# Matmul with rotary embedding on one core: how far ahead of the matmuls tiles are cast and transposed

## The chip, the cores and the metric

The kernel runs on one core of one Trainium2 chip. The metric is the device time of one execution in microseconds (us), taken as the median of several runs. Engines go by the profile's names: PE is TensorE (PEld its weight loads), DVE is VectorE, ACT is ScalarE, POOL is GpSimd, SP is SyncE, whose queue issues most loads. A "q" behind an engine's name is its sequencer, which issues DMAs and waits on semaphores.

## The reference

```python
batch, seq, hidden, n_heads = (16, 512, 768, 12)
y = np.matmul(x, weight)                       # x: 16 x 512 x 768, weight: 768 x 768, float32
y = y.reshape(batch, seq, n_heads, head_dim)   # head_dim = 64
y1, y2 = y[..., :32], y[..., 32:]
out1 = y1 * cos1 - y2 * sin1                   # cos, sin: seq x 64, halves taken the same way
out2 = y2 * cos2 + y1 * sin2
out = np.concatenate([out1, out2], axis=-1)    # back to 16 x 512 x 768
```

## The kernel before

**Tiles and pairs.** The 16 x 512 rows of x are cut into 64 tiles of 128 rows. Two tiles of the same rows in neighbouring batches make a pair, since they share their cosines and sines: 32 pairs (`NP`), pair n holding tiles 2n and 2n+1. In the main loop `i = 2 * n + s` is the tile whose matmuls are being issued.

**The way of a tile.** A tile of x is loaded, brought to float16 (the cast), transposed so that the 768 columns that are summed over lie on partitions (the "turn"), multiplied with the weights on PE into PSUM, multiplied on DVE with cosines and sines (`rope_bank`, line 187), added up on POOL (`add`, line 204) and stored (line 249). Loading, casting and transposing take one of three ways, by pair:

- Pairs 8, 12, 16, 20, 24 (`BLOCKS`): POOL's queue loads four quarters straight to float16 (`xh`, line 99), and DVE transposes them in blocks (line 148). There is no cast.
- Pairs 6, 10, 14, 18, 22, 26, 28 (`BLOCKS_SP`): SP's queue loads four quarters as float32 (`xf`, line 99), ACT casts each tile (line 76), and DVE transposes.
- All other pairs: SP's queue loads each tile (`xs`, line 83), ACT casts it, PE transposes it in six steps against an identity matrix (line 140) into PSUM (`pt`), and ACT copies that to SBUF (`xT`, line 76 again: one helper issues casts and copies).

So from pair 6 to pair 28 odd pairs go through PE and even ones through DVE.

**Order.** The kernel writes its own order (`manual_schedule`): on each engine instructions run in the order in which the code issues them. In the main loop, after the matmuls of tile i, `upto("turn", i + 3)` issues transpositions until those of all tiles below i+3 have been issued, and `upto("cast", i + 5)` does the same for casts; both do so once i is over 6 (before that, in pairs 2 and 3, calls with i+2 and i+4 stand between two halves of a tile's matmuls). For a tile that PE transposes, `turn` issues six transposes on PE and the copy on ACT; for the others, one transposition on DVE. Then come the products on DVE, and after the second tile of a pair the store of pair n-3 on ACT's queue and the addition of pair n on POOL. For the last four pairs (`ALONE`) the two `upto` calls stand before the tile's matmuls, and products, additions and stores go in smaller pieces.

**Loads and stores.** At pair n the SP queue is given the loads of pair n+5 and quarters of pairs n+5 to n+8. Buffers: 10 tiles of `xs`, 2 pairs of `xf`, 6 cast tiles `xc`, 8 transposed tiles `xT`, 2 PSUM banks for transposes and 6 for products, 3 pairs of products `tq`, 6 pairs of results `ov`. In the built program the DMAs of SP and ACT take eight completion semaphores in turn; each waits until the DMA that had its semaphore before has landed.

Of the kernel before, what the change touches and what calls it, by code (L numbers as in the profile page):

```python
# [17 lines left out]
def kernel(  # L18
# [21 lines left out]
    NP = B * SB // 2  # L40
# [46 lines left out]
    def load_pair(n):  # L87
        for s in (0, 1):
            if n < NP and n not in BLOCKS and n not in BLOCKS_SP:
                load(n, s)  # L90
# [10 lines left out]
    def load_blocks(n, quarters):  # L101
        if n not in BLOCKS:
            return
        if quarters[0] == 0:
            xhs[n] = bpool.tile([P, 2, H], FP16, tag="xh", name="xh")
            x16[n, 0], x16[n, 1] = xhs[n][:, 0], xhs[n][:, 1]
        for q in quarters:
            load_quarter(n, q, nc.gpsimd, xhs[n])

    def load_blocks_sp(n, q):  # L110
        if n not in BLOCKS_SP:
            return
        if q == 0:
            xhs[n] = hpool.tile([P, 2, H], FP32, tag="xf", name="xf")
            xss[n, 0], xss[n, 1] = xhs[n][:, 0], xhs[n][:, 1]
        load_quarter(n, q, nc.sync, xhs[n])
# [11 lines left out]
    def cast(n, s, eng):  # L128
        xc = cpool.tile([P, H], FP16, tag="xc", name="xc")
        x16[n, s] = xc  # L130
        src = xss.pop((n, s))
        src = src.rearrange("p (m t e) -> p t m e", t=NT, e=2)
        copy(eng, xc.rearrange("p (t m e) -> p t m e", t=NT, e=2), src)

    def transpose(n, s, eng):
        xc = x16.pop((n, s)).rearrange("p (t m e) -> p t e m", t=NT, e=2)
        bank = pt_pool.tile([P, 8, P], FP16, tag="pt", name="pt")
        pt = bank[:, 0 : 2 * NT].rearrange("p (t e) m -> p t e m", e=2)
        for t, e in CHUNKS:
            nc.tensor.transpose(pt[:, t, e, :], xc[:, t, e, :], ident)  # L140
        xT = tpool.tile([P, NT, 2, P], FP16, tag="xT", name="xT")
        copy(eng, xT, pt)
        xTT[n, s] = xT

    def transpose_blocks(n, s):
        order = "p (j a t) -> p t j a" if n in BLOCKS else "p (t j a) -> p t j a"
        xT = tpool.tile([P, NT, P, 2], FP16, tag="xT", name="xT")
        nc.vector.transpose(  # L148
            out=xT.bitcast(FP32).rearrange("p t (j a) o -> p t j (a o)", j=NQ),
            in_=x16.pop((n, s)).bitcast(FP32).rearrange(order, j=NQ, t=NT),  # L150
        )
        xTT[n, s] = xT.rearrange("p t m e -> p t e m")
# [4 lines left out]
    def psum(n, s):  # L157
        key, banks = (n, 3) if n < NP - ALONE else ((n, s), 2)
        if (n, s) == (NP - 1, 1):
            key, banks = (n, s), 3  # L160
        if key not in psys:
            psys[key] = [
                py_pool.tile([P, 512], FP32, tag="psy", name="psy") for _ in range(banks)
            ]
        ps = psys[key]
        if n >= NP - ALONE:
            cuts = (0, HH, H) if banks == 2 else (0, 5 * D, 10 * D, H)
            return [(b[:, 0 : hi - lo], lo, hi) for b, lo, hi in zip(ps, cuts, cuts[1:])]
        cut = 512 if s == 0 else 256
        return [(ps[s][:, ds(s * 256, cut)], 0, cut), (ps[s + 1][:, 0 : H - cut], cut, H)]  # L170

    def mm(n, s, t, e, c0=0, c1=H):
        for k, (ps, lo, hi) in enumerate(psum(n, s)):
            a, z = max(c0, lo), min(c1, hi)
            if a >= z:
                continue
            nc.tensor.matmul(  # L177
                ps[:, a - lo : z - lo],
                xTT[n, s][:, t, e, :],
                w_sb[:, t, e, a:z],  # L180
                start=((t, e) == CHUNKS[0] and n > 1),
                stop=((t, e) == CHUNKS[-1] and (n > 1 or s >= k)),
            )
# [11 lines left out]
    def rope(n, c0, c1, ps):  # L195
        if n not in tqs:
            tqs[n] = rpool.tile([P, 2, 2 * H], FP32, tag="tq", name="tq")
            ovs[n] = opool.tile([P, 2 * H], FP32, tag="ov", name="ov")
        products(n, ps, tqs[n][:, :, c0:c1])
# [11 lines left out]
    def rope_bank(n, b):  # L211
        rope(n, b * 512, (b + 1) * 512, psys[n][b])

    def add_pair(n, step=2 * H):
        for c in range(0, 2 * H, step):
            add(n, c, c + step, nc.gpsimd)
# [8 lines left out]
    def rope_last(n, ps, c0, c1):  # L225
        nh = (c1 - c0) // D
        q = tqs[n][:, 1, c0:c1]
        ph = ps.rearrange("p (h d) -> p h d", d=D)
        for o, j in ((q.rearrange("p (h d) -> p h d", d=D), 1), (ph, 0)):
            nc.vector.tensor_tensor(  # L230
                out=o, in0=ph, op=MULT,
                in1=csn[:, j, n % SB, :].unsqueeze(1).broadcast_to((P, nh, D)),
            )
        nc.vector.tensor_tensor(
            out=ovs[n][:, c0:c1].rearrange("p (h t d) -> p h t d", t=2, d=HD),
            in0=ps.rearrange("p (h t d) -> p h t d", t=2, d=HD),
            in1=q.rearrange("p (h t d) -> p h t d", t=2, d=HD)[:, :, ::-1, :],
            op=ADD,
        )

    def store(n, eng, c0=0, c1=2 * H):
        b, r = where(n, 0)
        dst = out.rearrange("b (p r) h -> r p b h", r=SB)[r, :, b : b + 2]
        src = ovs[n].rearrange("p (b h) -> p b h", b=2)
        if c1 - c0 < 2 * H:
            s = c0 // H
            dst = dst[:, s, c0 - s * H : c1 - s * H]
            src = src[:, s, c0 - s * H : c1 - s * H]
        eng.dma_start(out=dst, in_=src)
# [43 lines left out]
    def upto(what, k):  # L293
        while done[what] < min(k, 2 * NP):
            n, s = divmod(done[what], 2)
            done[what] += 1
            if what == "cast":
                if n not in BLOCKS:
                    cast(n, s, nc.scalar)
            elif n in BLOCKS or n in BLOCKS_SP:  # L300
                transpose_blocks(n, s)
            else:
                transpose(n, s, nc.scalar)
# [46 lines left out]
    for n in range(2, NP):  # L350
        load_pair(n + AHEAD - 2)
        for q, ahead in ((0, 8), (2, 7), (1, 6), (3, 5)):
            if n + ahead >= AHEAD:
                load_blocks_sp(n + ahead, q)
        for m, quarters in ((n + AHEAD_B, (0, 2)), (n + AHEAD_B - 1, (1, 3))):
            if m > BLOCKS[0]:
                load_blocks(m, quarters)
        for s in (0, 1):
            i = 2 * n + s
            if n < 4:  # L360

                for c0, c1 in ((0, 256), (256, H)):
                    for c in CHUNKS:
                        mm(n, s, *c, c0, c1)
                    if c0 == 0:
                        upto("turn", i + 2)
                        upto("cast", i + 4)
            elif n < NP - ALONE:
                for c in CHUNKS:
                    mm(n, s, *c)  # L370
            upto("turn", i + 3 if i > 6 else 0)
            upto("cast", i + 5 if i > 6 else 0)
            if n < NP - ALONE:
                for b in ((0,), (1, 2))[s]:
                    rope_bank(n, b)
                continue
            for ps, lo, hi in psum(n, s):
                for c in CHUNKS:
                    mm(n, s, *c, lo, hi)
                c0, c1 = s * H + lo, s * H + hi  # L380
                if (n, s, hi) == (NP - 1, 1, H):
                    rope_last(n, ps, c0, c1)
                    store(n, nc.sync, c0, c1)
                    continue
                rope(n, c0, c1, ps)
                if n >= NP - 2:
                    add(n, c0, c1, nc.gpsimd)
                elif hi == H:
                    add(n, s * H, (s + 1) * H, nc.gpsimd)
                if (n, s) == (NP - 1, 1):  # L390
                    if lo:
                        store(n, nc.scalar, s * H, c1)
                elif hi == H:
                    store(n, nc.sync, s * H, (s + 1) * H)
        if n < NP - ALONE:
            if n >= 3:
                store(n - 3, nc.scalar)
            add_pair(n, H if n >= NP - ALONE - 2 else 2 * H)
        if n == NP - ALONE - 1:
            for m in (n - 2, n - 1, n):  # L400
                store(m, nc.sync)
# [34 lines left out]
```

## Time and profile before

| | |
|---|---|
| time of five runs | 154.01 to 155.01 us, median 154.09 us |
| the profiled execution | 154.09 us, span 152.3 us |
| PE busy | 145.2 us, 95% of the span |
| DVE busy | 130.9 us, 86% |
| POOL busy | 123.7 us, 81% |
| ACT busy | 73.5 us, 48% |
| chain that ended last | PE 86%, POOL 7%, DVE 3% |
| matmuls (line 177) | 787 records, 131.4 us |
| transposes on PE (line 140) | 240, 20.3 us |
| copies `xT` on ACT | 38, 800 ns each |
| casts `xc` on ACT | 38 from `xs` at 904 ns, 14 from `xf` at 907 ns |
| transpositions on DVE (line 148) | 14 at 562 ns, 10 at 701 ns |
| granted PE clock | 1.00 in each stretch looked at between 16 and 140 us |
| data moved | 51.17 MB, 336 GB/s on average |

The span is the time from the first to the last instruction that the profile shows; the rest of the execution's time lies around it. Busy matmul time is that of records that overlap, so the sum over a row's instructions can be more than the row's busy time. A line such as "ACT xT L76 <- PE pt L140: 53.8, 34, 3.9" says that ACT's copies of line 76 waited for PE's transposes of line 140: 53.8 us in total, 34 times, 3.9 us at the longest. In a line of the chain the first number is the start in us, the second the duration, then engine, tile, line and count. In the timeline the bracket behind a row holds the engine's idle time before it and what ended that.

### The profile page before, as it was taken

What the parts mean: (1) busy time and instruction counts of PE and PEld (TensorE: products, weight loads), DVE (VectorE), ACT (ScalarE), POOL (GpSimd) and SP (SyncE); (2) the same over time, 40 slices, a digit from 0 to 9 for tenths busy, and PEclk for the clock granted to TensorE, in tenths of its full rate; (3) what the DMA queues carried; (4) which work ended last, traced back from release to release, by engine and by line L of the source; (5) the groups of instructions that cost most, each with busy time, mean ns of one, the idle gap of its engine ahead of it and who ended that gap; (6) DMA issues with size and microseconds to landing.
All of it is one profiled execution on the core that took longest, in us unless ns stands there. A gap on an engine that the chain in (4) does not pass through costs nothing.

```text
span 152.3 us, 2731 instructions
## 1 busy us (share of the span) xinstructions
PE 145.2 (95%) x1044; PEld 92.5 (61%) x1044; DVE 130.9 (86%) x141; ACT 73.5 (48%) x91; POOL 123.7 (81%) x69
## 2 busy tenths in 40 slices
PE   6999999999999999999999999999999999999950
PEld 2455678666656666666656666666656666666640
DVE  0566999779898989989898989989898989997890
ACT  3350696883534726282525624582616547764200
POOL 1000399999998999799997999787897879999990
PEclk9999999999999999999999999999999999999996
DMA  5999999999999999999999999999999999996554
GB/s 152 365 404 397 402 309 213 270 369 352 318 334 400 325 316 362 336 401 337 364 316 333 348 365 300 355 402 415 312 360 408 404 411 387 408 355 266 219 203 151
DMA packets 29037, 51.17 MB, mean 336 GB/s; under 512 B 7264, under 2 KB 14944, under 8 KB 29024
## 3 DMA queue, kind: packets, MB, share of 16 engines
q1 hardware_dynamic: 16640, 29.04, 56.7%
q10 hardware_dynamic: 6944, 19.99, 33.3%
q0 software_dynamic: 5440, 1.97, 10.7%
q8 instruction: 8, 0.13, 0.3%
q14 instruction: 5, 0.04, 0.1%
HBM read 27.79 MB, written 25.17 MB: 348 GB/s over the span
## 4 chain that ended last, share of the span: by engine, by line
PE 86%; POOL 7%; DVE 3%; POOLq 1%; issue 0%; DVEq 0%
PE psy L177 75%; PE pt L140 8%; POOL ov L204 7%; PE psy L259 3%; DVE tq L187 1%; DVE xT L78 1%; DVE xc L78 1%; POOLq L431 1%; DVE cold L266 0%; DVE w_sb L126 0%; POOLq L204 0%; DVEq L187 0%
## 5 line engine op out<-in xcount | busy, mean ns | idle before, releaser
L177 PE MATMUL psy<-w_sb,xT 128*128 128x256 f16 (+3 forms) x787 | 131.4, 322 | 0.2 <-DVE w_sb L126 0.2
L187 DVE TENSOR_TENSOR tq<-psy,csn 128x1024 f32<-128x1024 f32 (+2 forms) x100 | 112.1, 1163 | 9.5 <-PE psy L177 9.1
L204 POOL TENSOR_TENSOR ov<-tq 128x1536 f32<-128x1536 f32 (+3 forms) x42 | 111.5, 2680 | 7.9 <-DVE tq L187 5.2
L177 PEld LDWEIGHTS <-xT 128*128 128x128 f16 x787 | 75.2, 98 | 44.8 <-ACT xc L76 0.5
L76 ACT COPY xT<-pt 128x768 f16<-128x768 f16 x38 | 30.4, 800 | 57.9 <-PE pt L140 53.8
L76 ACT CAST xc<-xs 128x768 f16<-128x768 f32 x38 | 33.0, 904 | 9.7 <-DMA xs<-in_x_dram 7.6
L140 PEld LDWEIGHTS <-xc 128*128 128x128 f16 x240 | 17.0, 99 | 6.0 <-DVE xc L78 1.1
L140 PE MATMUL pt<-ident,xc 128*128 128x128 f16 x240 | 20.3, 221 | 0.3 <-DVE xc L78 0.3
L336 POOL COPY mark<-xs 128x1 f32<-128x1 f32 x1 | 0.2, 184 | 16.0 <-DMA xs<-in_x_dram 16.0
L76 ACT CAST xc<-xf 128x768 f16<-128x768 f32 x14 | 12.7, 907 | 0.0
L99 POOL DMA_DIRECT2D xh<-in_x_dram x20 | 11.8, 595 | 0.5 <-issue 0.5
L148 DVE STREAM_TRANSPOSE xT<-xc 128x384 f32<-128x384 f32 x14 | 7.9, 562 | 0.0
L259 PE MATMUL psy<-cold 128*128 128x512 f16 x17 | 6.5, 533 | 1.2 <-DVE cold L266 1.2
L148 DVE STREAM_TRANSPOSE xT<-xh 128x384 f32<-128x384 f32 x10 | 7.0, 701 | 0.0
L126 DVE CAST w_sb<-w_raw 128x768 f16<-128x768 f32 (+2 forms) x7 | 3.4, 501 | 1.9 <-DMA w_raw<-in_weight_dram 1.9
L78 DVE CAST xc<-xs 128x768 f16<-128x768 f32 x2 | 1.9, 947 | 2.9 <-DMA xs<-in_x_dram 2.9
L259 PEld LDWEIGHTS <-cold 128*128 128x128 f16 x17 | 2.0, 131 | 3.5 <-issue 2.2
L78 DVE COPY xT<-pt 128x768 f16<-128x768 f16 x2 | 1.1, 558 | 1.9 <-PE pt L140 1.9
L76 ACT ACT_TABLE_LOAD x1 | 1.3, 1283 | 0.7 <-PEq L417 0.7
L266 DVE MEMSET cold<- 128x256 uint32 x1 | 0.3, 272 | 0.9 <-PEq L417 0.9
L267 POOL MEMSET ident<- 128x128 f16 x1 | 0.2, 204 | 0.3 <-POOLq L417 0.3
L331 DVE COPY csn<-sin_sb 128x128 f32<-128x128 f32 x1 | 0.2, 226 | 0.2 <-DMA sin_sb<-in_sin_dram 0.2
(9 smaller groups left out, 1.8 us busy)
## 6 DMA issues: line engine op xcount, KB each, us to landing
out_dram<-ov ACTq DMA_DIRECT2D x25, 768.0 KB, 8.5
xs<-in_x_dram SPq DMA_DIRECT2D x40, 384.0 KB, 9.0
xf<-in_x_dram SPq DMA_DIRECT2D x28, 192.0 KB, 10.7
out_dram<-ov SPq DMA_DIRECT2D x7, 384.0 KB, 2.3
out_dram<-ov SPq DMA_DIRECT2D x3, 768.0 KB, 6.2
w_raw<-in_weight_dram SPq DMA_DIRECT2D x5, 384.0 KB, 6.8
xh<-in_x_dram POOLq DMA_DIRECT2D x20, 96.0 KB, 10.1
out_dram<-ov ACTq DMA_DIRECT2D x1, 320.0 KB, 2.2
```

The source lines that it names most:

```text
L76: eng.copy(out=o, in_=i_)
L78: eng.tensor_copy(out=o, in_=i_)
L99: eng.dma_start(out=dst[ts(q, R)], in_=src[r, q])
L126: nc.vector.tensor_copy(out=w_sb[:, t, e, c0:c1], in_=w_raw[t, e][:, c0:c1])
L140: nc.tensor.transpose(pt[:, t, e, :], xc[:, t, e, :], ident)
L148: nc.vector.transpose(out=xT.bitcast(FP32).rearrange("p t (j a) o -> p t j (a o)", j=NQ), in_=x16.pop((n, s)).bitcast(FP32).rearrange(orde ...
L177: nc.tensor.matmul(ps[:, a - lo : z - lo], xTT[n, s][:, t, e, :], w_sb[:, t, e, a:z], start=((t, e) == CHUNKS[0] and n > 1), stop=((t, e) ...
L187: nc.vector.tensor_tensor(out=tq.rearrange("p j (h d) -> p j h d", d=D), in0=ps.rearrange("p (h d) -> p h d", d=D) .unsqueeze(1).broadcast ...
L204: eng.tensor_tensor(out=ovs[n][:, ds(c0, w)].rearrange("p (h t d) -> p h t d", t=2, d=HD), in0=tq[:, 0].rearrange("p (h t d) -> p h t d", ...
L259: nc.tensor.matmul(psys[n][b], cold[:, 0:P], cold, start=True, stop=opened[0] < WARM - 6)
L266: nc.vector.memset(cold, 0.0)
L431: with _tile.TileContext(nc) as tc:
```

## The change

The two `upto` calls of the main loop get a lead that depends on the tile:

```diff
                 for c in CHUNKS:
                     mm(n, s, *c)
-            upto("turn", i + 3 if i > 6 else 0)
-            upto("cast", i + 5 if i > 6 else 0)
+
+            lead = 1 if i < 2 * NP - 20 else 0
+            upto("turn", i + 3 + lead if i > 6 else 0)
+            upto("cast", i + 5 + 2 * lead if i > 6 else 0)
             if n < NP - ALONE:
```

`2 * NP - 20` is 44. For i from 7 to 43 transpositions are issued up to tile i+3 instead of i+2 and casts up to tile i+6 instead of i+4. From i = 44, which begins the last ten pairs, the limits are those of before; the counters stand at tiles 46 and 49 by then, so the next transposition is issued at i = 45 and the next cast at i = 46. At i = 7, where the lead begins, two transpositions (tiles 9 and 10) and three casts (tiles 11, 12, 13) are issued together, where there were one and one. Nothing else in the kernel is changed; `upto` skips casts of pairs that need none.

## The prediction

> **What bounds the kernel now.** I read the waits of TensorE first, then the chain that ended last, then ScalarE's timeline where the change begins, then the queue of loads.
>
> ```profile
> span 152.3 us, 2731 instructions
> PE psy L259 <- DVE cold L266: 1.2, 1, 1.2
> PE pt L140 <- DVE xc L78: 0.3, 1, 0.3
> PE psy L177 <- DVE w_sb L126: 0.2, 1, 0.2
> ...
> 25.69 0.34 PE pt L140 x6
> 26.03 1.29 PE psy L177 x6
> 27.32 0.34 PE pt L140 x6
> 27.66 1.95 PE psy L177 x12
> ...
> 135.28 1.87 DVE tq L187 x2
> ...
> 130.56 18.16 POOL L204 TENSOR_TENSOR ov<-tq 128x768 f32<-128x768 f32 x14 [0.31 <-POOL ov L204]
> ```
>
> The three waits are all that TensorE has, and the timeline puts each of them before 9.2 us. From there to 146.9 us it strings 1.95 us of matmuls per tile and 0.34 us of transposes per tile of an odd pair without a hole. Pairs 6 to 28 alternate, so two pairs take 8 x 0.975 + 2 x 0.34 = 8.47 us, 4.23 a pair. The tail hangs on it: DVE's products of pair 27 follow its last matmul at 129.3, GpSimd's additions start at 130.56 and run 18.16 us without idling to 148.72, and one store and the end follow (152.3). ScalarE is busy 48% of the span. Its waits show where it has room:
>
> ```profile
> ACT xT L76 <- PE pt L140: 53.8, 34, 3.9
> ACT xc L76 <- DMA xs<-in_x_dram: 7.6, 2, 4.6
> ACT xT L76 <- DMA xf<-in_x_dram: 4.1, 1, 4.1
> ```
>
> 53.8 us are copies waiting for TensorE, and only the last row (and one of 2.0) is a stall on a DMA in the body.
>
> **The change part by part.** No instruction is added or removed: both kernels build to the same number on every engine. Three things move. Below, T(k) is the transposition of tile k (line 140 on TensorE, 148 on DVE) and i the tile whose matmuls the loop is at.
>
> *The step at i=7.* Here the lead jumps, and tile 7 gets T(9), T(10) and the casts of 11, 12, 13 at once, where it had T(9) and cast 11. ScalarE's own order there was:
>
> ```profile
> 26.06 0.80 ACT L76 COPY xT<-pt 128x768 f16<-128x768 f16 x1 [0.70 <-PE pt L140]
> 26.76 0.92 ACT L76 CAST xc<-xs 128x768 f16<-128x768 f32 x1
> 27.69 0.80 ACT L76 COPY xT<-pt 128x768 f16<-128x768 f16 x1
> 27.78 0.42 ACTq L249 DMA_DIRECT2D out_dram<-ov  x1
> 28.39 0.90 ACT L76 CAST xc<-xs 128x768 f16<-128x768 f32 x1
> ```
>
> These are the copy of 8, the cast of 10, the copy of 9, the store of pair 0 and the cast of 11. TensorE finishes T(9) at 27.16 + 0.34 = 27.49 and now has T(10) next, whose cast ends at 27.68. From a cast's end to its first transpose the trace shows 0.06 (DVE's cast 6.79 + 0.94, transposes at 7.79), so T(10) starts at 27.74: 0.25 us of stall. T(10) takes 0.34, tile 8's matmuls 1.95: 30.03. T(11) needs cast 11, which now stands behind the copy of 10. Rows follow each other on ScalarE at 0.70 for a copy: 27.69, copy of 10 at 28.39, cast 11 from 29.09 to 29.99, release 30.05: 0.02. **Sum 0.27 us**. The trace has no T(10) here. Its bounds are 0, if the cast ends 0.25 us sooner, and 0.52, if both waits cost the 0.26 that stands before the transposes at 7.79. A gain is excluded: TensorE's work is the same, and it has no idle time after 9.2 us to give back. I take 0.27.
>
> Behind it, casts 12 and 13 wait for the last quarter of pair 6, which landed at 30.40 in the trace. They run 30.4 to 32.1, and the copy of 11 to about 32.9. Tile 11's matmuls start at 34.3, so 1.4 us of cover remain; past it each us of a late landing is a us of TensorE. The store of pair 0 goes out at about 31.3 instead of 27.78. GpSimd wants its buffer back at pair 6, about 43.3; with the longest landing of a store, 11.0 us, it is there at 42.3.
>
> *Casts two tiles earlier, pairs 6 to 23.* A cast waits for its load, and on ScalarE the copies and stores stand behind it. SyncE's and ScalarE's DMAs share eight completion semaphores in turn, and nearly every one is issued the moment the one eight before it lands (pair 15's second tile at 52.83, its predecessor landed at 52.81), so loads can't simply come 4.2 us earlier. How near they are, from the landings of the trace: the last quarter of pair 10 at 44.40, cast at 47.67; of pair 14 at 60.71, cast at 64.61; pair 15 at 63.82, cast from 67.69; pair 18 at 77.11, cast at 81.65; pair 23 at 95.33, cast from 101.57. With two tiles (about 4.2 us) less, ScalarE meets several loads that have not landed. Tile 28 (pair 14): T(23) ends about 55.9 instead of 57.6, its copy starts at 56.0, casts 26 and 27 run to 58.4, and cast 28 would wait to 60.71, so 2.3 us. What hides it: the copy behind it is of T(26), which TensorE does at 61.8 and which is needed by tile 26's matmuls at 66.1 + 0.27 = 66.4. So cast 28 may start as late as 66.4 - 0.8 - 0.9 = 64.7, 4.0 us after that landing. Cost 0.
>
> Take it from a rule instead: the Trainium skill ("DMA: Bandwidth & Descriptors", section "Rules for kernel authors") says to issue a DMA early, compute, and wait on its semaphore late; this change waits earlier. Counting the 2.3 us above as lost, the rule would make the sum 154.09 + 0.27 + 2.3 = 156.7 for one such cast. The row speaks for 154.4, because a copy with 4.0 us to spare stands between the waiting cast and TensorE.
>
> *Stores.* In ScalarE's new order the store of an even pair from pair 4 on stands behind a copy and follows TensorE: pair 4's goes from 41.39 to about 46.2, pair 8's from 58.41 to about 63.0, pair 6's from 52.00 to about 54.0; odd pairs' stay within a us or go earlier. GpSimd needs the buffers six pairs on: pair 10's addition at 59.9 against 46.2 + 11.0 (longest landing) = 57.2, pair 14's at 76.8 against 74.0. So 2.7 us of cover; without it GpSimd, with 3.47 us of additions and on average 0.6 of DMA issues in 4.23, has 0.16 a pair to recover. A late store also holds its semaphore: pair 4's now stands ahead of pair 15's second tile, which goes from 52.83 to about 46.2 + 10 = 56 and lands near 67, where its cast is due at about 66. Other loads gain: with the store of pair 0 out of the way those of pairs 7 to 10 are issued up to 2.7 us earlier (pair 7's second tile at 20.3, when its new predecessor lands, instead of 22.99). I take these as cancelling.
>
> *Transposes one tile earlier.* On TensorE the same 0.34 us in another place: 0. On DVE a transposition (0.56 or 0.70 us) now stands ahead of an even pair's second bank, where DVE idled 0.40 to 0.67 us for TensorE, so that bank starts 0 to 0.3 us later. GpSimd took pair 8 at 51.83 with its products done at 51.0: hidden.
>
> *Last ten pairs.* From tile 44 on the old order stands, since T is at 46 and casts at 49 already. The tail only shifts: 0.
>
> The profiled execution took 154.09 us (span 152.3 and 1.8 around it), which is also the median of the five. **154.09 + 0.27 = 154.4 us.**
>
> **Rivals.**
>
> *The loads don't follow (slower).* Mechanism: ScalarE's in-order queue behind a cast on a late load, with stores behind it that hold semaphores that later loads wait for. For it: margins of 3.3 to 6 us lose 4.2, the DMA share is at its top in slices 2 to 36, and landings spread widely:
>
> ```profile
> DMA  5999999999999999999999999999999999996554
> ...
> xs<-in_x_dram SPq DMA_DIRECT2D x40, 384.0 KB, 9.0
> DMA to landing us min/median/max: 7.0/10.7/13.5
> ```
>
> (the last row is that of pair 6's to 28's quarters). Against it: 4.0 us of cover, and a lap from one cast through the store behind it to the load that waits for it and that load's cast is five pairs at the shortest (pair 10 to pair 15), 21.2 us, where medians ask 0.9 + 8.5 + 9.0 = 18.4 and the longest 0.9 + 11.0 + 14.2 = 26.1. It decides once a load lands over 4.0 us later than now. Price: a quarter at 13.5 instead of 10.7 (2.8) plus the 3.4 of a held semaphore is 6.2, less 4.0 = 2.2 us of stall, once, since the stall gives the loads time: 154.4 + 2.2 = 156.6; between 154.9 and 157.
>
> *The step costs nothing.* Cast 10 ends in time or the other kernel's rows stretch less: 154.1, or 154.0 where copies that were just in time (one started at 90.46 where its matmuls began at 91.52) had cost something in other executions.
>
> *Faster by over 0.5%.* It would need 0.77 us out of TensorE's unbroken 137.7 or of GpSimd's 18.16 in the tail; no row shows where. 153.2.
>
> **How the numbers follow.** Forecast 0.62 (154.2 to 154.6), no cost 0.12 (154.0 to 154.1), loads late 0.21, faster 0.05. Within 0.5% (0.77 us, about what a measurement of this kernel can tell from no change) lie the first two, 0.74; slower 0.21; faster 0.05. The range of 153.8 to 155.8 takes in the bounds 0 and 0.52 and the milder half of late loads; it leaves out some 0.04 below and 0.11 above.
>
> **What would show it.** Right: TensorE's waits gain one of about 0.25 us <- ScalarE's cast near 27.7 and next to nothing else, pair 14's first matmul about 0.3 us later, ScalarE waits for xf or xs rise by several us, GpSimd's tail still 18.2 us. Wrong: TensorE waiting on xT anywhere after 34 us (late loads), GpSimd waiting for its buffers, or a tail that starts earlier than 130.5.

## The result, and the profile after

| | before | changed |
|---|---|---|
| median | 154.53 us (95 executions) | 154.93 us (53 executions) |
| lowest and highest | 153.85 to 156.71 us | 154.18 to 157.08 us |
| the profiled execution | 154.09 us, span 152.3 us | 154.59 us, span 152.4 us |
| time outside the span, median | 1.79 us | 2.16 us |
| PE busy | 145.2 us | 144.8 us |
| GpSimd's tail | 18.16 us from 130.56 | 18.16 us from 130.74 |

The changed kernel takes 1.0028 times as long, 95% interval 1.0017 to 1.004. That is 0.43 us (0.26 to 0.62), which lies within the 0.5% called no change. Of the gap of 0.50 us between the two profiled executions only 0.17 us lies in the span (152.27 to 152.44 by the trace's records); the rest lies outside it. Executions more than 1.5% above the fastest of their kernel (four of the kernel before, one of the changed one) are left out of the medians and counts of spans below.

The page of the changed kernel, its first line:

```profile
span 152.4 us, 2725 instructions
```

Six instructions fewer than the 2731 of before. None of them computes or moves data (PE has 1044 matmuls in both, DVE 141 instructions, ACT 91); what is missing are instructions that only wait on semaphores. This line turns out to matter.

The chain that ended last, changed kernel, at the tile where the lead begins (start, duration, engine, tile, line, count; "issue" is time with no wait shown):

```profile
24.95 0.66 PE psy L177 x6
25.60 0.35 PE pt L140 x6
...
26.67 0.92 ACT xc L76
27.59 0.05 issue
27.64 0.51 PE pt L140 x6
28.15 1.95 PE psy L177 x12
```

In the kernel before, the chain stayed on PE through this stretch. Now it leaves PE for ScalarE's cast of tile 10, which ends at 27.59, and comes back with the transposes of tile 10 at 27.64. The timeline of PE's weight loads in the same stretch has the wait in its bracket:

```profile
26.85 0.54 PEld L140 LDWEIGHTS <-xc 128*128 128x128 f16 x6
27.63 0.34 PEld L140 LDWEIGHTS <-xc 128*128 128x128 f16 x6 [0.24 <-ACT xc L76]
27.93 1.78 PEld L177 LDWEIGHTS <-xT 128*128 128x128 f16 x12
```

Start to start, the matmul records have a hole of 0.233 us there, the only one of more than 0.03 us after 18 us. Three later transposes (the second of tile 10, the first two of tile 11) start 0.011 to 0.013 us late each, so that PE takes 119.81 us from the first transpose of tile 9 to its last matmul, where it took 119.54 us before: 0.27 us more. That the two spans differ by less comes from the start: the transposes of tile 9 began 0.09 us earlier in this execution. The list of all waits, changed kernel (total us, times, longest):

```profile
ACT xT L76 <- PE pt L140: 53.4, 32, 3.8
...
ACT xc L76 <- DMA xs<-in_x_dram: 9.3, 5, 4.8
...
POOL ov L204 <- DVE tq L187: 6.2, 10, 1.1
...
ACT xc L76 <- DMA xf<-in_x_dram: 2.3, 2, 1.1
...
PEld L140 <- ACT xc L76: 0.9, 3, 0.4
```

ScalarE's casts of `xf` tiles now wait in the body, where before they did not (the row of these casts, first before, then changed; the last column is the idle time before them):

```profile
L76 ACT CAST xc<-xf 128x768 f16<-128x768 f32 x14 | 12.7, 907 | 0.0
L76 ACT CAST xc<-xf 128x768 f16<-128x768 f32 x14 | 12.6, 907 | 3.5 <-DMA xf<-in_x_dram 2.3
```

The other 1.2 of the 3.5 us stand under `xs` in the list of waits (9.3 us instead of 7.6; its longest, 4.8 us, is at the start). Yet no row has PE waiting for `xT`, the copies behind those casts. ScalarE's timeline shows where the longest of these waits are and what became of the stores:

```profile
31.02 0.89 ACT L76 CAST xc<-xf 128x768 f16<-128x768 f32 x1 [1.13 <-DMA xf<-in_x_dram]
31.07 0.42 ACTq L249 DMA_DIRECT2D out_dram<-ov  x1
...
42.52 0.89 ACT L76 CAST xc<-xf 128x768 f16<-128x768 f32 x1 [1.15 <-DMA xf<-in_x_dram]
...
45.16 0.40 ACTq L249 DMA_DIRECT2D out_dram<-ov  x1
...
59.27 0.89 ACT L76 CAST xc<-xf 128x768 f16<-128x768 f32 x1 [0.90 <-DMA xs<-in_x_dram]
...
62.80 0.38 ACTq L249 DMA_DIRECT2D out_dram<-ov  x1
```

Three casts in the body wait 0.90 to 1.15 us, and the stores of pairs 0, 4 and 8 go out at 31.07, 45.16 and 62.80 (27.78, 41.39 and 58.41 before). GpSimd's row for the tail is what it was, 0.18 us later:

```profile
130.74 18.16 POOL L204 TENSOR_TENSOR ov<-tq 128x768 f32<-128x768 f32 x14 [0.31 <-POOL ov L204]
```

So inside the span there is one loss, at the step, of 0.27 us in all, and spans of many executions don't even show that: their median is 152.8 us for the kernel before (84 executions) and 152.8 us for the changed one (65). The 0.43 us by which the times differ are nearly the 0.37 us by which the time outside the span has grown. Two questions follow. Where do the 0.27 us go, if the spans agree? And what sets the time outside?

### The profile page after: what moved, and what is told of

It is laid out like the page before. It is cut to its first block, busy times and chain, and to the rows that moved or that the text cites. A ratio compares the mean times of both kernels' runs of the same rounds, so it can differ in the third digit from the quotient of the medians.

```text
span 152.4 us, 2725 instructions
## 1 busy us (share of the span) xinstructions
PE 144.8 (95%) x1044; PEld 91.8 (60%) x1044; DVE 132.0 (87%) x141; ACT 73.7 (48%) x91; POOL 123.8 (81%) x69
## 4 chain that ended last, share of the span: by engine, by line
PE 80%; POOL 7%; DMA 5%; SPq 2%; DVE 2%; issue 1%; ACT 1%; POOLq 1%; DVEq 0%
PE psy L177 73%; PE pt L140 7%; POOL ov L204 7%; DMA w_raw<-in_weight_dram 5%; DVE tq L187 1%; SPq L123 1%; SPq L83 1%; ACT xc L76 1%; POOLq L433 1%; DVE w_sb L126 0%; POOLq L204 0%; ACT xT L76 0%; DVEq L187 0%
## 5 line engine op out<-in xcount | busy, mean ns | idle before, releaser
L76 ACT COPY xT<-pt 128x768 f16<-128x768 f16 x38 | 30.3, 799 | 55.9 <-PE pt L140 53.4
L76 ACT CAST xc<-xs 128x768 f16<-128x768 f32 x38 | 33.0, 905 | 8.2 <-DMA xs<-in_x_dram 8.1
L140 PEld LDWEIGHTS <-xc 128*128 128x128 f16 x240 | 16.3, 98 | 6.6 <-DVE xc L78 1.6
L76 ACT CAST xc<-xf 128x768 f16<-128x768 f32 x14 | 12.6, 907 | 3.5 <-DMA xf<-in_x_dram 2.3
L259 PE MATMUL psy<-cold 128*128 128x512 f16 x17 | 5.9, 489 | 1.2 <-DVE cold L266 1.2
```

The source lines that it names most:

```text
L76: eng.copy(out=o, in_=i_)
L259: nc.tensor.matmul(psys[n][b], cold[:, 0:P], cold, start=True, stop=opened[0] < WARM - 6)
```

## The experiments

The theory at the outset: the step at i=7 costs 0.23 us, the rest of the lead costs nothing or gains a little, and something outside the span adds 0.37 us. The rivals: the lead itself costs time in the body, by casts behind late loads; or the time outside comes from the new order of loads and stores. Spans below are medians, with their lowest and highest in brackets; "outside" is an execution's time less its span. Ratios are against the kernel before on the same chip.

### The lead begins two tiles later

At i=9 the step issues the transposes of tile 11 and, on DVE, the transposition of tile 12; cast 10 is done by then. Everything else is as in the change.

```diff
-            lead = 1 if i < 2 * NP - 20 else 0
+            lead = 1 if 8 < i < 2 * NP - 20 else 0
```

> The change with its start moved: the lead begins at tile 9 instead of tile 7 (8 < i < 44), so T(10) and T(11) stay one to a tile on TensorE and the second transposition of the step is DVE's T(12). Step theory (the whole cost is TensorE's wait of 0.24 us for cast 10 at the step): the wait is gone, ratio to the kernel before 1.000 (0.9985 to 1.0015), tail within 0.1 us of before once the start-up is taken off. Late-loads rival (casts in the body meet loads that have not landed, or late stores hold back loads and buffers, in part of the executions): the cost stays, 1.002 to 1.004.

Measured: 154.66 us, ratio 0.9989 (0.9967 to 1.0011); span 152.5 us (152.1 to 152.7) against 152.9 us (152.0 to 154.3) of the kernel before; outside 2.16 us. PE's weight loads at the place in question:

```profile
27.39 0.54 PEld L140 LDWEIGHTS <-xc 128*128 128x128 f16 x6
27.89 1.78 PEld L177 LDWEIGHTS <-xT 128*128 128x128 f16 x12
29.79 0.43 PEld L140 LDWEIGHTS <-xc 128*128 128x128 f16 x6
```

There is no bracket any more: without transposes of tile 10 behind those of tile 9, nothing waits. So the wait is the step's, as predicted, and it goes when the step is moved. From tile 9's transposes to its last matmul PE takes 119.54 us, as in the kernel before, and so it does in the two further profiles of this order below. In these executions the lead costs nothing and gains nothing. (This profile's span of 152.7 us is long because those transposes start at 27.61 us; over all twelve profiles that start lies between 27.07 and 27.77 us, with the lead and without.) Yet the median span of this order lies 0.4 us below that of before. The gain would then come from executions in which the old order loses time that its profile, a short execution, doesn't show; a shorter start-up in these runs isn't excluded. The time outside stays at 2.16 us although the step has gone.

### One half of the change at a time

```diff
 # casts only
-            upto("turn", i + 3 + lead if i > 6 else 0)
+            upto("turn", i + 3 if i > 6 else 0)
 # transposes only
-            upto("cast", i + 5 + 2 * lead if i > 6 else 0)
+            upto("cast", i + 5 if i > 6 else 0)
```

> Only the casts get the lead, the transpositions stay at i+3. Step theory: no T(10) behind T(9), so the 0.24 us at 27.6 are gone; but the copy of tile 10 now stands behind casts 12 and 13, whose last quarter lands at 30.4 to 31.0, so it starts at 32.0 to 32.7 instead of 29.98 and ends at 32.8 to 33.4, while tile 10's matmuls were due at 32.06: a stall of 0.8 to 1.4 us there, ratio 1.005 to 1.009. If ScalarE's order does not carry the wait to TensorE: 1.000. Late-loads rival: beyond that, stalls in the body, above 1.010.

Measured: 155.13 us, ratio 1.0033 (1.0002 to 1.0063); span 153.35 us (152.6 to 154.6); outside 1.79 us. ScalarE's timeline where the lead begins, casts only:

```profile
28.42 0.90 ACT L76 CAST xc<-xs 128x768 f16<-128x768 f32 x1
30.14 0.90 ACT L76 CAST xc<-xf 128x768 f16<-128x768 f32 x1 [0.81 <-DMA xf<-in_x_dram]
30.94 0.89 ACT L76 CAST xc<-xf 128x768 f16<-128x768 f32 x1
31.74 0.78 ACT L76 COPY xT<-pt 128x768 f16<-128x768 f16 x1
```

The copy of tile 10 stands behind the casts of 11, 12 and 13, and 12 waits for its load. Tile 10's matmuls come at 32.58 with 0.48 us of hole before them, start to start. The expectation was larger because the load landed earlier here than in the profile of before. A second hole, 0.45 us at 83.35, was not expected; there the casts of tiles 36 and 37 stand behind two stores, at 80.85 and 81.50, and the copy that PE needs stands behind the casts. Early casts alone put the copies late: it is the transposes and copies one tile earlier that give the casts their cover.

> Only the transpositions get the lead, the casts stay at i+5. Step theory: T(10) still follows T(9) at tile 7 and waits 0.24 us for cast 10, so the same cost as the change, ratio 1.0015 to 1.003, and no ScalarE waits on loads in the body. Late-loads rival: no cast is earlier, so no cost, 1.000.

Measured: 155.48 us, ratio 1.0034 (1.0001 to 1.0067); span 153.0 us (152.4 to 153.8); outside 2.15 us. The profiled execution was one of the longest of its kernel (157.12 us) and is read for its mechanism alone; it says nothing of how often this happens. It has the expected hole of 0.23 us at 27.73, and two that were not expected, 0.39 us at 70.19 and 1.72 us at 87.53. The last, in PE's timeline and then in ScalarE's:

```profile
89.47 0.51 PE L140 MATMUL pt<-ident,xc 128*128 128x128 f16 x6 [1.56 <-ACT xc L76]
```

```profile
88.05 0.38 ACTq L249 DMA_DIRECT2D out_dram<-ov  x1
88.53 0.89 ACT L76 CAST xc<-xs 128x768 f16<-128x768 f32 x1 [2.16 <-DMA xf<-in_x_dram]
```

Transposes a tile earlier are a tile closer to their casts, and a cast that is held up is then late for PE. What held this one, of tile 38, isn't its load, which had landed at 78.07, but the store in front of it: the store's semaphore came free at 87.97, when a load of pair 21 landed. The hole at 70.19 has a store at 69.36 in front of the cast in the same way. So in these profiles neither half is a gain by itself: the casts need the earlier copies, and the transposes need the earlier casts.

### The lead to the end

```diff
-            lead = 1 if i < 2 * NP - 20 else 0
+            lead = 1
```

> The lead is kept to the end, also in the last ten pairs. Step theory: the end adds nothing, since the transpositions of tiles 58 to 63 only change places with matmuls of GpSimd's 18.16 us tail, which starts with pair 27 and runs 0.5 us behind: the same as the change, 1.002 to 1.004. Rival (late stores): casts of pairs 26 and 28 wait 2 to 5 us for quarters that land at 111.8 and 119.3, stores 20 to 24 behind them go out later, and GpSimd, which had 2 us to spare for pair 21's buffer, waits: 0.5 to 2 us more, 1.006 to 1.015.

Measured: 154.74 us, ratio 0.9995 (0.9967 to 1.0023); span 152.95 us (152.6 to 153.9); outside 1.79 us. The step's hole is there, 0.23 us. GpSimd's tail, which was expected unchanged, isn't:

```profile
130.89 8.96 POOL L204 TENSOR_TENSOR ov<-tq 128x768 f32<-128x768 f32 x5 [0.30 <-POOL ov L204]
140.25 1.82 POOL L204 TENSOR_TENSOR ov<-tq 128x768 f32<-128x768 f32 x1 [0.41 <-DVE tq L187]
```

It runs from 130.89 to 149.46, 18.57 us, because GpSimd waits 0.41 us for DVE's products in the middle of it. In this profile, then, ending the lead at i=44 is worth 0.41 us. And the time outside the span is 1.79 us, as before, with the lead and its step in place: the 0.37 us don't come from the lead as such, and without them the ratio is lower by 0.0024 than it would be.

### The time outside the span

By now six kernels, the two of the case and four of the experiments, had two values outside the span, and they sorted by one thing: how many instructions DVE's program has, waits counted (a profile records two fewer: 190 before, 189 changed). The kernel before and those with 1.79 us have 192, the changed one and the others with 2.16 us have 191. To test it, one tiny instruction is put on DVE at the start, where it is not waited for long:

```diff
+    spare = konst.tile([P, 1], FP32)
 ...
     nc.vector.memset(cold, 0.0)
+    nc.vector.memset(spare, 0.0)
```

It is added to the change, to the order that begins at i=9, and to the kernel before; a fourth kernel takes the one instruction of this kind off DVE in the kernel before (`nc.vector.memset(cold, 0.0)` becomes `nc.gpsimd.memset(cold, 0.0)`).

> The change, with one instruction more on DVE: a memset of a spare 128x1 tile that nothing reads, right behind the first memset. DVE's program then has 192 instructions as before the change, instead of 191. So far the device time was 1.79 us above the span in every execution of the three kernels with 192 (before, casts alone, lead to the end) and 2.16 us in every one of the three with 191 (the change, start at tile 9, transposes alone). Program-length theory: 1.79 outside the span, span unchanged at 152.8, ratio 0.999 to 1.001 where the change had 1.0028. Rival (the 0.37 us come from the order that the change makes): 2.16 outside, ratio 1.002 to 1.004.

> The lead begins at tile 9 and DVE has the spare memset (192 instructions). If the cost of the change is the 0.24 us of TensorE at the step and 0.37 us outside the span, and its lead in the body takes away waits that the kernel before has in many executions, this one beats both: span 152.5, 1.79 outside, 154.3 us, ratio 0.997 to 0.999. Rival (the body gains nothing): span as before, ratio 1.000.

> The kernel before, with the memset of the warm-up tile on GpSimd instead of DVE, so that DVE's program has 190 instructions; nothing else. Program-length theory: 2.16 us outside the span, the span within 0.1 of before, ratio 1.0015 to 1.0035, with no lead at all. Rival (the change's order makes it): 1.79, ratio 1.000.

> The kernel before with the spare memset on DVE: 193 instructions. If it is a threshold at 192, 1.79 us outside the span and ratio 1.000; if exactly 192 is the good length (a multiple of 16 or 64, say), 2.16 and 1.002. The profile is also a further look at the kernel before: the body theory expects TensorE waits of some tenths of a us after 34 us in part of its executions (its spans go from 152.0 to 155.9 us, those with the lead from tile 9 from 152.1 to 152.7).

Measured:

| kernel | DVE's program | median | ratio (95%) | span | outside |
|---|---|---|---|---|---|
| change, one more | 192 | 154.84 us | 1.004 (1.0005 to 1.0074) | 153.05 (152.6 to 154.7) | 1.76 us |
| from i=9, one more | 192 | 154.17 us | 0.9988 (0.9961 to 1.0015) | 152.4 (152.0 to 153.5) | 1.77 us |
| before, one less | 190 | 156.07 us | 1.0098 (1.006 to 1.0136) | 154.0 (152.6 to 154.7) | 2.02 us |
| before, one more | 193 | 154.91 us | 1.0026 (0.9993 to 1.0059) | 153.0 (152.3 to 153.9) | 1.94 us |

An instruction that does nothing for the result takes 0.4 us off the time outside, twice. With 190 and 193 it is 2.02 and 1.94 us, which neither of the numbers written down beforehand names: that the time outside goes with DVE's count is shown for 191 and 192, that it knows only two values is wrong, and why it goes with it is open. For 190 GpSimd's program also became one longer, so there the two can't be told apart. The first and third kernels were not as short as expected, because their spans came out longer: the change with one more by 0.25 us (its profile has three waits at the start of 0.18, 0.37 and 0.32 us for the weights' conversion and the same 0.23 us at the step), the kernel before with one less by 1.2 us, for which its profile, one of its shorter executions, gives no reason but a hole of 0.15 us at 83.0 behind a store at 81.83.

The fourth kernel's profile is worth more than its time. It is the order of before, caught in a longer execution (span 153.5 us; lines are shifted by one). ScalarE's timeline:

```profile
91.26 0.38 ACTq L250 DMA_DIRECT2D out_dram<-ov  x1
91.73 1.50 ACT L77 COPY xT<-pt 128x768 f16<-128x768 f16 x2 [4.83 <-PE pt L141]
```

and PE's:

```profile
91.20 0.50 PE L141 MATMUL pt<-ident,xc 128*128 128x128 f16 x6
92.59 1.69 PE L178 MATMUL psy<-w_sb,xT 128*128 128x512 f16 x9 [0.89 <-ACT xT L77]
```

The store stands ahead of the copies on ScalarE's queue. It is issued at 91.26, because the load that had its semaphore before, a quarter of pair 22, landed at 91.18. The first of the two copies could have started some 2 us earlier: its transposes ran on PE from 88.92 to 89.42, and ScalarE had been idle since 86.9. The bracket names PE's later transposes as the releaser, but those are the second copy's; what held the first is the store in front. PE, which needs the first copy for its next tile, waits until 92.59, 1.05 us start to start. In the profile of before the same store and copy were

```profile
89.98 0.38 ACTq L249 DMA_DIRECT2D out_dram<-ov  x1
90.46 0.80 ACT L76 COPY xT<-pt 128x768 f16<-128x768 f16 x1 [4.12 <-DMA xf<-in_x_dram]
```

The quarter landed at 89.91, the store went at 89.98, the copy ran from 90.46 to 91.26, and the matmuls began at 91.35: the cover was less than 0.1 us. The lead adds a tile's matmuls, 1.95 us, to that cover, since the copy that PE needs next may then be made a tile earlier. The profile of the changed kernel has a case in which this helped:

```profile
82.66 0.38 ACTq L249 DMA_DIRECT2D out_dram<-ov  x1
83.14 0.80 ACT L76 COPY xT<-pt 128x768 f16<-128x768 f16 x1 [2.44 <-PE psy L177]
```

The transposes of this copy, of tile 35, had ended at 81.28, so the store held it for 1.86 us; tile 35's matmuls began at 85.01, without a hole.

### Once more, side by side

The order from i=9 with one more instruction had come out below both kernels, though not clearly. It and the changed kernel ran again on one chip.

> The lead from tile 9 with 192 instructions on DVE once more, on whichever chip it falls. If it beats both kernels: span 152.4 with little spread (152.0 to 152.7 but for single executions), 1.77 outside, 154.2 us, below the kernel before in this call by 0.2 to 0.5 us; if the first result was luck, the same as before.

> The change as it is, beside the other on the same chip, to set the two spans against each other. Step theory: span 0.24 us above that of the lead from tile 9 (the wait for cast 10), 2.16 outside, so 0.6 us above it in time; its profile again with one wait of 0.23 us near 27.5 and none after 34 us. Rival (the step is hidden by something later): equal spans, 0.37 us in time.

Measured: from i=9 with one more 154.26 us, ratio 0.9958 (0.9933 to 0.9984), span 152.45 us (152.1 to 152.6), outside 1.79 us; the changed kernel 155.03 us, ratio 1.0006 (0.9981 to 1.0032), span 152.85 us (152.5 to 153.9), outside 2.15 us. Between the two lie 0.77 us: 0.4 in the span and 0.36 outside it. This version of the change beats both kernels, the one before by 0.42% in this run and by 0.12% in the run above, whose interval includes 1; both are within the 0.5% called no change.

The profiled execution of the changed kernel was a longer one this time (156.1 us, span 153.9). The step's hole is 0.229 us at 27.85, and there is one that was not expected. ScalarE's timeline, then PE's:

```profile
85.14 0.38 ACTq L249 DMA_DIRECT2D out_dram<-ov  x1
85.62 0.80 ACT L76 COPY xT<-pt 128x768 f16<-128x768 f16 x1 [4.37 <-PE psy L177]
```

```profile
86.47 1.80 PE L177 MATMUL psy<-w_sb,xT 128*128 128x256 f16 x10 [0.80 <-ACT xT L76]
```

It is the same pattern as in the order of before. The store waits for its semaphore, which a quarter of pair 22 frees by landing at 85.07; the copy behind it is of transposes that PE made from 81.28 to 81.78; and PE loses 0.96 us. The tile of lead is not enough here, since the store held ScalarE for more than 3 us after those transposes. So the lead doesn't end it. Spans above 153.25 us were 23 of 84 for the kernel before, 8 of 65 for the changed kernel and 1 of 36 for the order from i=9 (three runs of it together, two of them with the spare instruction, median 152.4 us). With the two other kernels that have one more instruction on DVE counted to their orders, they were 28 of 96 for the old order and 12 of 77 for the changed one. Long spans are thus rarer with the lead; that a late store made each of them isn't shown, since only two of them, one of either order, were profiled among the kernels counted here.

## Why the prediction held, step by step

*What bounds the kernel.* Right. PE has no hole of more than 0.03 us after 28 us in the profiled execution, and the tail is 18.16 us again.

*The step at i=7.* Right in place, cause and size: 0.25 us predicted for tile 10's transposes, 0.233 measured before the first and 0.011 before the second; for tile 11's about 0.02 predicted, 0.025 measured. The sum of 0.27 us is also what PE takes longer from tile 9's transposes to its last matmul (119.54 to 119.81 us). Moved by two tiles, it is gone. The bound of 0.52 us, both waits at the longer release, was not needed.

*Casts two tiles earlier.* Right. ScalarE did wait for loads, 1.13, 1.15 and 0.90 us (2.3 had been allowed for tile 28's cast), and none of it reached PE. The rule to issue a DMA early and to wait on its semaphore late (the Trainium skill, "DMA: Bandwidth & Descriptors", section "Rules for kernel authors"), taken as a price for waiting earlier as the prediction took it, would have charged such waits; the profile charges none, since what stands behind the waiting cast on its engine was not needed yet. Where it was, the rule holds: the casts-only kernel has a waiting cast ahead of a copy that PE is about to use, and loses 0.48 us.

*Stores.* Pair 0 predicted at 31.3, pair 4 at 46.2, pair 6 at 54.0 and pair 8 at 63.0; measured 31.07, 45.16, 54.06 and 62.80. Pair 15's second tile was to go at 56 and land near 67, and went at 54.59 and landed at 63.56. GpSimd never waited for its buffers. In that execution late stores cost nothing; the second profile, with 0.96 us at 85.4, shows that the rival "the loads don't follow" was no idle one: PE waits on `xT` after 34 us there, which the prediction had named as a sign of being wrong. Its point of decision is a store's semaphore rather than a cast on a late load. The profile of before had a hint of this: the 4.1 us of "ACT xT L76 <- DMA xf", which the prediction read as a stall on a load, are those of the copy at 90.46, which reads `pt` and no load and stands behind the store at 89.98.

*Transposes earlier on DVE, and the last ten pairs.* No cost, right. That the lead ends has a value that the prediction didn't see: with the lead to the end GpSimd's tail gained a wait of 0.41 us.

*The sum.* The predicted 154.4 us is 0.5 us below the measured 154.93 us. Most of that is the starting point, the median of five executions (154.09 us) instead of that of 95 (154.53); the increase itself was 0.43 us instead of 0.27. Two steps under the sum were wrong, in opposite directions. That they nearly cancel is luck.

The first is "No instruction is added or removed: both kernels build to the same number on every engine". That is so for instructions that work, not for those that only wait: DVE's program went from 192 to 191 and the page's count from 2731 to 2725. With it the "1.8 around it" was carried over as a constant, where it is 2.16 us for the changed kernel: 0.37 us, more than the term that was worked out.

The second is "A gain is excluded: TensorE's work is the same, and it has no idle time after 9.2 us to give back". This was read from one execution, and a short one: its span of 152.3 us lies 0.5 us under the median of 152.8, and its time of 154.09 us 0.44 us under the median of 95 executions. In a longer one the old order does lose time to a late store, 1.05 us at once, as the kernel with one more instruction showed. The rival "the step costs nothing" had this in half a sentence (copies that were just in time may have cost something in other executions), at 0.1 us instead of about 0.4: the spans with the lead from i=9 have a median of 152.4 us against 152.8.

Together: 0.37 us outside and 0.27 at the step, less about 0.4 in the body by the spans of the order from i=9, would make some 0.2 us more; measured are 0.43 us (0.26 to 0.62) by the times and 0.37 by the medians of the spans and the time around them. The changed kernel's median span lies 0.4 us above that of the order from i=9, of which the step explains 0.27. Among the spans under 153.25 us the means are 152.70 and 152.41 us, 0.29 apart, so there the step is all; what is left falls to the longer spans (8 of 65 against 1 of 36). One of these 8 was profiled and has a late store; for the others that isn't shown.

## What to carry to other kernels

Let the lead of a software pipeline begin where the work it pulls forward is already done: the same change begun two tiles later has no wait at the step. Ask of a wait what stands behind it on its in-order queue, not how long it is: here casts waited over a microsecond at no cost, while a store's wait for a semaphore ahead of one copy cost PE a microsecond. And before a few tenths of a microsecond are explained, split the time into span and rest, and look at the spread of the spans: a single profile can be a good execution of a kernel that often has worse ones.

## What the runs showed of the hardware

**Time outside the span goes with the number of instructions on DVE.** With 190, 191, 192 and 193 instructions on DVE it was 2.02, 2.16, 1.79 and 1.94 us; the values of the kernels with 191 (2.10 to 2.22 us) and with 192 (1.74 to 1.88 us) don't overlap, whatever the order in the body. In the records behind the span four of five blocks of semaphore clears begin 0.33 to 0.37 us later in the changed kernel than in the kernel before, counted from the span's end (one of them at 1.19 us instead of 0.82), and the fifth at 0.66 us in both; so it is the end that stretches. With 190, where GpSimd's program changed too, one block alone is late, at 1.27 us. Other engines' counts changed too (ScalarE's from 206 to 201), but only DVE's sorts the values of 1.79 and 2.16 us. Why is open.

**Short waits of PE don't show as idle time of PE.** A matmul record of a 512-column product lasts 379 ns while the next begins 217 ns after it, so a hole of less than about 0.16 us vanishes under modelled ends. A transpose's record lasts 219 ns and the next begins 56 ns after it, so of the 0.233 us at the step 0.07 are left between records; they appear as 0.24 us on the weight loads and in no row of PE. The Trainium skill ("Perfetto Trace Analysis", section "Tensor Engine Instruction (MATMUL, LD_WEIGHTS)") says that the end of a matmul in a profile is computed from the instruction's size and a delay, not observed, which agrees with these rows. The prediction's sentence that three waits are all that PE has holds for that view alone; start to start, the profile of before has two more holes of over 0.1 us, 0.18 us at 11.9 and 0.17 us at 17.6.

**A store on an engine's queue is part of that engine's order.** Its wait for a completion semaphore holds the copy behind it (landing at 91.18, store at 91.26, copy at 91.73, matmuls at 92.59 in the order of before with one more instruction). Stores on another queue would show what this is worth in all; it was not tried.
